# A hybrid decoder step on one core: the mixer's branches in another order, and its vector work in smaller steps

## Chip, core and metric

The kernel runs on one core of a Trainium2 chip. The metric is the device time of one execution in microseconds. Before the change three runs gave 2646.72, 2648.06 and 2648.72; the median is 2648.06.

## What is computed

One inference step of a two-layer trunk over 512 prompt tokens and 8 sequences of 8 sample tokens (576 columns), width 1024, in fp32. Each layer has a SwiGLU half step, a mixer and a second SwiGLU half step, each behind an RMS norm with scale and shift from a conditioning vector. The mixer, cut to what matters:

```python
xa, bg, cg, u, v, p, ga, gb, gc = split(h @ w_in)
y_a = (bg * conv3(concat(hist, cg * xa))) @ w_out_a              # conv branch
v   = layernorm(gelu(v)) * ln_g
y_b = (gelu(u) * (tril(w_s) @ v + b_s)) @ w_out_b                # gated MLP, chunks of 128
y_c = grouped(trailing_mean_w(p) - p) * pool_scale               # pool, w = 2, 4, 8, 16
out = (sigmoid(ga) * y_a + sigmoid(gb) * y_b + sigmoid(gc) * y_c) @ w_o
```

New conv, pool and v rows are outputs too.

## The kernel before

Activations lie with features on partitions and the 576 tokens as two halves of 288 columns (256 prompt, 32 sample). Every fp32 product is made of three fast ones: each operand is split into a rounded high part and the remainder, and `wlo*hi`, `whi*lo`, `whi*hi` are summed in a PSUM bank (lines 474 to 477). Five banks rotate first in, first out.

A **unit** (`units`, line 464) is one output tile of 128 x 288: its matmuls, then its evacuation, then `beat()`. A **group** (`Groups.group`, line 736) makes four output tiles by a scheme of seven products of 12 matmuls instead of eight; the bank of each product is copied or added by ScalarE (`pd`, `pe`, `pu`) and VectorE, and the seventh product, the tail, is issued within the next group or by `flush`. After each product `gone()` runs one `beat()`, one step of weight preparation (`W.go`) and a `tick`.

The order of the work is the order of the program: each engine takes its instructions in turn. Two lists delay work: `later(n, f)` runs `f` n beats on, and `after(n, f)` n ticks on (a product counts half a tick). So a step that waits for another engine holds back all that stands behind it on its own engine.

Weights come by DMA from the SP queue in pieces of up to 1 MB into two raw buffers, in the order of the list `raws` (lines 162 to 234), and are split ahead of use into six slots. A piece for a group needs two sums on GpSimd (L366, L362), two differences on VectorE (L362) and four splits (ScalarE L325, then VectorE L329). Other pieces are split by ScalarE and VectorE, every third by GpSimd (L323, L329), by a running count.

The mixer (`mixer`, line 995) does, per layer: v and u with layernorm (each 128-token block is transposed into a bank, normalised by VectorE with a power on GpSimd, and multiplied by `ln_g`); then the gated MLP: gate groups GB and, between them, outputs (`ypair`), whose evacuation starts the accumulator `acc`; then conv: groups XA, CG, BG, gate groups GA and outputs whose product is added to `acc` by GpSimd (L1163); then pool: groups PP, and gate groups GC0, GC2, GC4, GC6, between whose products the pool outputs `yc` (three matmuls each) are placed by `hook`. Each pool output is multiplied by its gate (L1440), added to `acc` (L1444) and split into `mgh` (ScalarE, L1446) and `mgl` (VectorE, L1447), which feed the product with `w_o` in `end_stage`. During a mixer the residual x lies in DRAM; its buffers hold split operands of the groups, and x is read back (L1480) at the mixer's end. While `pool_w` is in use its slot (`pw`) is not free.

Of the kernel before, what the change touches and what calls it, by code (L numbers as in the profile page):

```python
# [35 lines left out]
def kernel(  # L36
# [113 lines left out]
    colc = cp.tile([P, 88], F32, name="colc")  # L150
# [57 lines left out]
    for l in range(DEPTH):  # L208
        add_ffn(w1_gu[l], w1_dn[l], CHUNKS[l][0])
        wi = w_in[l]  # L210
        for c in (VV, VV + 256, UU, UU + 256):
            add_cols(wi, c, KT)
        for g, out in ((GB, w_out_b[l]), (GA, w_out_a[l])):
            if g == GA:
                for c in (XA, CG, XA + 256, CG + 256, BG, BG + 256):
# [9 lines left out]
        add_st(wi, PP)  # L225
        add_st(wi, PP + 256)
        add_st(wi, GC)
        add_pool(pool_w[l])
        add_st(wi, GC + 256)
        add_st(wi, GC + 512)  # L230
        add_st(wi, GC + 768)
# [232 lines left out]
    def units(specs, hooks={}, late=False, w=1):  # L464
# [23 lines left out]
        beat()  # L488
# [506 lines left out]
    def mixer(l, nxt):  # L995
# [36 lines left out]
        def layernorm(n):  # L1032
# [13 lines left out]
            rs = tmp("bnrs", 1, 2)  # L1046
            nc.vector.tensor_scalar_add(rs[:R], mv[:R, 1:2], EPS)
            nc.gpsimd.tensor_tensor(out=rs[:R], in0=rs[:R], in1=mhalf[:R, :1], op=ALU.pow)
            t = vn[n] = alloc(F32, "vn")
            nc.vector.tensor_scalar(t[:R, :512], bk[:R], mv[:R, 0:1], rs[:R], ALU.subtract, ALU.mult)  # L1050
            nc.vector.tensor_mul(t[:R, :512], t[:R, :512], lng[:R, :512])
            if n == 4:
                nc.sync.dma_start(o_nv[l].rearrange("b t c -> (b t) c"), t[:64, :512])
                release(vs, lng, *[v[m] for m in range(4)])
# [51 lines left out]
        def gating(hp):  # L1106
# [8 lines left out]
            for e in range(2):  # L1115
# [7 lines left out]
            nc.vector.tensor_add(  # L1123
                tg3[:, :, :PH].rearrange("p h (n t) -> p h n t", n=2),
                bk.rearrange("p (h n t) -> p h n t", h=2, n=2),
                bc.unsqueeze(1).unsqueeze(1).to_broadcast([P, 2, 2, P]))
# [30 lines left out]

        def evac_ya(m, h):
            def e(ps):
                t = sg.pop((m, h))  # L1160
                nc.vector.tensor_mul(t, ps[:, :HALF], t)
                a = acc[m][:, h * HALF:(h + 1) * HALF]
                nc.gpsimd.tensor_add(a, a, t)  # L1163
                qrelease(t)
            return e

        def ypair(rhs, evac, m):
            s = W.take()
            for h in (0, 1):
                for i in (0, 1):  # L1170
# [13 lines left out]
        hsc = alloc(F32, "hsc")  # L1184
        nc.sync.dma_start(hsc[:16, :512], state_conv[l].rearrange("b k c -> (b k) c"))
# [8 lines left out]


        xa, ext, cv = {}, {}, {}
        exs = alloc(F32, "exs")
        exs4 = exs[:, :320].rearrange("p (m s t) -> p m s t", m=4, s=8)
        def conv_hist():
            bk = tpbank()  # L1200
            for m in range(4):
                nc.tensor.transpose(bk[:, m * 16:(m + 1) * 16], hsc[:16, m * P:(m + 1) * P],
                                    ident[:16, :16])
            nc.vector.tensor_copy(
                exs4[:, :, :, 0:2], bk[:, :64].rearrange("p (m s t) -> p m s t", m=4, s=8))
            release(hsc)

        after(2, conv_hist)
        ncol = tmp("ncol", 4 * 18, 1)
        ncol3 = ncol.rearrange("p (m c) -> p m c", m=4)  # L1210

        def evac_xa(m, h):
            def e(ps, own=None):
                if own is None:
                    own = qalloc("xa")
                    nc.scalar.activation(own, ps[:, :HALF], AF.Copy)
                xa[m, h] = own
            return e

        def evac_cg(m, h):  # L1220
            def e(ps, own=None):
                first = m not in ext
                if first:
                    ext[m] = alloc(F32, "ext")
                    nc.gpsimd.memset(ext[m][:, 0:2], 0.0)
                a = xa.pop((m, h))
                nc.vector.tensor_mul(ext[m][:, 2 + h * PH:2 + (h + 1) * PH], ps[:, :PH], a[:, :PH])
                nc.vector.tensor_mul(exs4[:, m, 4 * h:4 * h + 4, 2:10],
                                     ps[:, PH:HALF].rearrange("p (s t) -> p s t", s=4),
                                     a[:, PH:HALF].rearrange("p (s t) -> p s t", s=4))  # L1230
                qrelease(a)
                if own is not None:
                    qrelease(own)
                if not first:
                    conv(m)
            return e

        def conv(m):

            cv[m] = alloc(F32, "cv")  # L1240
            w = [colc[:, 48 + (l * 3 + k) * 4 + m:48 + (l * 3 + k) * 4 + m + 1] for k in range(3)]
            o = cv[m].rearrange("p (h c) -> p h c", h=2)[:, :, 0:PH]
            os_ = cv[m].rearrange("p (h c) -> p h c", h=2)[:, :, PH:HALF].rearrange(
                "p h (s t) -> p h s t", s=4)
            e_ = lambda k: ext[m][:, k:k + 512].rearrange("p (h c) -> p h c", h=2)
            s_ = lambda k: exs4[:, m, :, k:k + 8].rearrange("p (h s) t -> p h s t", h=2)

            def tap0():
                nc.scalar.activation(o, e_(0), AF.Copy, scale=w[0])
                nc.vector.tensor_scalar_mul(os_, s_(0), w[0])  # L1250

            def tap(k):
                nc.vector.scalar_tensor_tensor(out=o, in0=e_(k), scalar=w[k], in1=o,
                                               op0=ALU.mult, op1=ALU.add)
                nc.vector.scalar_tensor_tensor(out=os_, in0=s_(k), scalar=w[k],
                                               in1=os_, op0=ALU.mult, op1=ALU.add)

            def last():
                nc.gpsimd.tensor_copy(ncol3[:, m, 0:2], ext[m][:, 512:514])
                nc.gpsimd.tensor_copy(ncol3[:, m, 2:18].rearrange("p (s t) -> p s t", s=8),  # L1260
                                      exs4[:, m, :, 8:10])
                release(ext[m])

            tap0()
            later(1, lambda: tap(1))
            later(2, lambda: (tap(2), last()))

        yah, yal, cvn = {}, {}, {}

        def evac_bg(m, h):  # L1270
            def e(ps, own=None):
                if m not in yah:
                    yah[m], yal[m] = alloc(F32R, "yah"), alloc(F32R, "yal")
                g = qalloc("g32") if own is None else own
                c = slice(h * HALF, (h + 1) * HALF)
                nc.vector.tensor_mul(g, ps[:, :HALF], cv[m][:, c])
                cvn[m] = cvn.get(m, 0) + 1
                if cvn[m] == 2:
                    release(cv[m])
                hi, lo = yah[m][:, c], yal[m][:, c]  # L1280

                def low():
                    nc.vector.tensor_sub(lo, g, hi.bitcast(F32))
                    qrelease(g)

                def high():
                    nc.scalar.activation(hi, g, AF.Copy)
                    later(1, low)
                later(1, high)
            return e  # L1290

        def out_conv():
            bk = tpbank()
            for m in range(4):
                nc.tensor.transpose(bk[:18, m * P:(m + 1) * P], ncol3[:, m, :], ident)
            t = alloc(F32, "ncv")
            nc.scalar.activation(t[:18, :512], bk[:18], AF.Copy)
            nc.sync.dma_start(o_ncp[l, 0], t[0:2, :512])
            nc.sync.dma_start(o_ncs[l].rearrange("b k c -> (b k) c"), t[2:18, :512])
            release(t)  # L1300

        for m in (0, 2):
            G.group(evac_xa, m)
            G.group(evac_cg, m)
        after(5.5, out_conv)
        G.group(evac_bg, 0)
# [542 lines left out]
```

## Time and profile before

| | us |
|---|---|
| median of three runs | 2648.06 |
| profiled execution | 2651.93 |
| its span | 2650.2 |
| TensorE busy | 2531.8 |
| VectorE busy | 1815.5 |
| ScalarE busy | 1125.9 |
| GpSimd busy | 867.5 |
| mean granted clock | 0.983 |

A share of the whole span is a mean over stages. The stages of the two mixers are read from windows: the first mixer's lie between 485 and 924 us, the second's between 1783 and 2225. The clock column there is the granted share of TensorE's full clock.

### The profile page before, as it was taken

What the parts mean: (1) busy time and instruction counts of PE and PEld (TensorE: products, weight loads), DVE (VectorE), ACT (ScalarE), POOL (GpSimd) and SP (SyncE); (2) the same over time, 40 slices, a digit from 0 to 9 for tenths busy, and PEclk for the clock granted to TensorE, in tenths of its full rate; (3) what the DMA queues carried; (4) which work ended last, traced back from release to release, by engine and by line L of the source; (5) the groups of instructions that cost most, each with busy time, mean ns of one, the idle gap of its engine ahead of it and who ended that gap; (6) DMA issues with size and microseconds to landing.
All of it is one profiled execution on the core that took longest, in us unless ns stands there. A gap on an engine that the chain in (4) does not pass through costs nothing. (4 is left out here: it accounts for less than half of the span.)

```text
span 2650.2 us, 46656 instructions
## 1 busy us (share of the span) xinstructions
PE 2531.8 (96%) x18604; PEld 2423.4 (91%) x18604; DVE 1815.5 (69%) x3167; ACT 1125.9 (42%) x2094; POOL 867.5 (33%) x942
## 2 busy tenths in 40 slices
PE   7999999999997999999999999999999879999998
PEld 5889999889997889999989999998999879999998
DVE  5766666766868586666776666767686765776675
ACT  4434334444444263334444344444444443453453
POOL 1223334312243323333443332452122514233241
PEclk8999999999999999999999999999999989999999
DMA  7554533312222424442324444241223231132222
GB/s 230 195 182 157 191 104 130 94 63 88 84 88 68 147 73 149 153 151 96 112 81 160 163 159 148 85 132 63 89 80 107 66 136 48 64 100 91 97 76 80
DMA packets 264761, 303.51 MB, mean 115 GB/s; under 512 B 10957, under 2 KB 224253, under 8 KB 264527
## 3 DMA queue, kind: packets, MB, share of 16 engines
q1 hardware_dynamic: 264542, 300.52, 34.2%
q8 instruction: 147, 2.41, 0.4%
q14 instruction: 72, 0.58, 0.1%
HBM read 292.74 MB, written 7.97 MB: 113 GB/s over the span
## 5 line engine op out<-in xcount | busy, mean ns | idle before, releaser
L329 DVE TENSOR_TENSOR wlo<-raw,whi 128x1024 fp32r<-128x1024 f32 (+2 forms) x548 | 631.8, 1161 | 231.0 <-ACT whi L325 222.4
L727 PE MATMUL mm<-hhi,wlo 128*128 128x288 f32 x1920 | 575.1, 300 | 35.0 <-ACT pe L765 34.2
L325 ACT ACTIVATE whi<-raw 128x1024 fp32r<-128x1024 f32 (+2 forms) x548 | 467.6, 861 | 318.4 <-PE mm L477 115.7
L728 PE MATMUL mm<-hlo,whi 128*128 128x288 f32 x1920 | 569.8, 297 | 0.0
L729 PE MATMUL mm<-hhi,whi 128*128 128x288 f32 x1920 | 569.7, 297 | 0.0
L727 PEld LDWEIGHTS mm<-hhi,wlo 128*128 128x128 f32 x1920 | 363.0, 189 | 61.4 <-ACT pe L765 39.3
L474 PE MATMUL mm<-ghi,wlo 128*128 128x288 f32 x1408 | 418.5, 297 | 0.0
L477 PE MATMUL mm<-ghi,whi 128*128 128x288 f32 x1408 | 415.1, 295 | 0.0
L476 PE MATMUL mm<-glo,whi 128*128 128x288 f32 x1408 | 414.8, 295 | 0.0
L729 PEld LDWEIGHTS mm<-hhi,whi 128*128 128x128 f32 x1920 | 363.1, 189 | 0.0
L728 PEld LDWEIGHTS mm<-hlo,whi 128*128 128x128 f32 x1920 | 363.1, 189 | 0.0
L727 PE MATMUL mm<-thi,wlo 128*128 128x288 f32 x1120 | 332.6, 297 | 1.6 <-ACT pd L754 1.6
L728 PE MATMUL mm<-tlo,whi 128*128 128x288 f32 x1120 | 330.3, 295 | 0.0
L729 PE MATMUL mm<-thi,whi 128*128 128x288 f32 x1120 | 329.5, 294 | 0.0
L366 POOL TENSOR_TENSOR whi<-raw 128x512 f32<-128x512 f32 x120 | 171.8, 1432 | 480.2 <-DMA raw<-in_w_in_dram 189.8
L802 DVE SCALAR_TENSOR_TENSOR x<-mm,mod,x 128x256 f32<-128x256 f32 x336 | 161.2, 480 | 222.4 <-PE mm L477 222.3
L474 PEld LDWEIGHTS mm<-ghi,wlo 128*128 128x128 f32 x1408 | 264.3, 188 | 17.8 <-issue 16.8
L476 PEld LDWEIGHTS mm<-glo,whi 128*128 128x128 f32 x1408 | 264.2, 188 | 0.2
L477 PEld LDWEIGHTS mm<-ghi,whi 128*128 128x128 f32 x1408 | 264.2, 188 | 0.0
L727 PEld LDWEIGHTS mm<-thi,wlo 128*128 128x128 f32 x1120 | 210.1, 188 | 14.1 <-issue 5.0
L729 PEld LDWEIGHTS mm<-thi,whi 128*128 128x128 f32 x1120 | 210.6, 188 | 0.0
L810 POOL TENSOR_TENSOR x<-x,t 128x32 f32<-128x32 f32 x240 | 112.2, 468 | 300.3 <-DVE t L805 297.8
(316 smaller groups left out, 4949.4 us busy)
## 6 DMA issues: line engine op xcount, KB each, us to landing
raw<-in_w_gu_dram SPq DMA_DIRECT2D x88, 1024.0 KB
ada<-in_w_ada_dram SPq DMA_DIRECT2D x256, 256.0 KB
raw<-in_w_in_dram SPq DMA_DIRECT2D x48, 1024.0 KB
raw<-in_w_dn_dram SPq DMA_DIRECT2D x52, 512.0 KB
raw<-in_w_dn_dram SPq DMA_DIRECT2D x24, 768.0 KB
adap<-in_w_ada_dram SPq DMA_DIRECT2D x32, 256.0 KB
raw<-in_w_o_dram SPq DMA_DIRECT2D x8, 1024.0 KB
xd<-x SPq DMA_DIRECT2D x16, 288.0 KB
```

The lines of the kernel that those rows point to most:

```text
L325: nc.scalar.activation(hi, src, AF.Copy)
L329: eng.tensor_sub(lo, src, hi.bitcast(F32))
L366: nc.gpsimd.tensor_add(v4(self.sums[r][0])[:, 0], a21, a22)
L474: nc.tensor.matmul(o, wlo, rhi, start=(k == 0), stop=False)
L476: nc.tensor.matmul(o, whi, rlo, start=False, stop=False)
L477: nc.tensor.matmul(o, whi, rhi, start=False, stop=(k == K - 1 and not late))
L727: nc.tensor.matmul(o, wlo, rhi, start=(start and k == 0), stop=False, skip_group_check=True)
L728: nc.tensor.matmul(o, whi, rlo, start=False, stop=False, skip_group_check=True)
L729: nc.tensor.matmul(o, whi, rhi, start=False, stop=(k == 3), skip_group_check=True)
L802: nc.vector.scalar_tensor_tensor(out=xc, in0=ps[:, :PH], scalar=mod[:, gidx + m, 0:1], in1=xc, op0=ALU.mult, op1=ALU.add)
L810: (nc.gpsimd if late else nc.vector).tensor_add(xs, xs, t)
```

## The change

The order of the branches becomes gated MLP, pool, conv; the weight list follows. Layernorm's scaling is done by ScalarE one beat after the statistics, and `ln_g` is multiplied in at the gating, as a column, for the prompt blocks. The split of the gated result is made in two later beats. Pool outputs no longer count as beats (`still`) and are added to `acc` by GpSimd; the last four are placed in the first conv group. The conv outputs add `acc` on GpSimd and make `mgh` and `mgl` in three beats. x is read back before the last eight conv outputs. The four outputs of a `ypair` come tile by tile instead of half by half.

```diff
-            nc.vector.tensor_scalar(t[:R, :512], bk[:R], mv[:R, 0:1], rs[:R], ALU.subtract, ALU.mult)
-            nc.vector.tensor_mul(t[:R, :512], t[:R, :512], lng[:R, :512])
...
+            def scale():
+                nc.vector.scalar_tensor_tensor(out=rs[:R, 1:2], in0=mv[:R, 0:1], scalar=-1.0,
+                                               in1=rs[:R, 0:1], op0=ALU.mult, op1=ALU.mult)
+                t = vn[n] = alloc(F32, "vn")
+                nc.scalar.activation(t[:R, :512], bk[:R], AF.Identity, scale=rs[:R, 0:1],
+                                     bias=rs[:R, 1:2])
...
+            later(1, scale)
```

Gating:

```diff
-            nc.vector.tensor_add(
-                tg3[:, :, :PH].rearrange("p h (n t) -> p h n t", n=2),
...
+            for h in range(2):
+                nc.vector.scalar_tensor_tensor(
+                    out=tg3[:, h, :PH].rearrange("p (n t) -> p n t", n=2),
+                    in0=bk[:, h * PH:(h + 1) * PH].rearrange("p (n t) -> p n t", n=2),
+                    scalar=colc[:, 88 + l * 4 + hp:88 + l * 4 + hp + 1],
+                    in1=bc.unsqueeze(1).to_broadcast([P, 2, P]), op0=ALU.mult, op1=ALU.add)
...
-            nc.scalar.activation(ybh[hp], tg, AF.Copy)
-            nc.vector.tensor_sub(ybl[hp], tg, ybh[hp].bitcast(F32))
-            release(tg)
+            def low():
+                nc.vector.tensor_sub(ybl[hp], tg, ybh[hp].bitcast(F32))
+                release(tg)
+            def high():
+                nc.scalar.activation(ybh[hp], tg, AF.Copy)
+                later(1, low)
+            later(1, high)
```

Conv outputs and pool outputs:

```diff
         def evac_ya(m, h):
...
-                a = acc[m][:, h * HALF:(h + 1) * HALF]
-                nc.gpsimd.tensor_add(a, a, t)
-                qrelease(t)
+                def add():
+                    nc.gpsimd.tensor_add(t, t, acc[m][:, c])
...
+                def high():
...
+                    nc.scalar.activation(mgh[m][:, c], t, AF.Copy)
+                def low():
+                    nc.vector.tensor_sub(mgl[m][:, c], t, mgh[m][:, c].bitcast(F32))
+                    qrelease(t)
+                for n, f in enumerate((add, high, low)):
+                    later(n + 1, f)
...
         def evac_yc(m, h):
...
-                nc.vector.tensor_add(t, t, a)
-                hi = mgh[m][:, h * HALF:(h + 1) * HALF]
-                nc.scalar.activation(hi, t, AF.Copy)
-                nc.vector.tensor_sub(mgl[m][:, h * HALF:(h + 1) * HALF], t, hi.bitcast(F32))
-                qrelease(t)
+                def add():
+                    a = acc[m][:, h * HALF:(h + 1) * HALF]
+                    nc.gpsimd.tensor_add(a, a, t)
+                    qrelease(t)
+                later(1, add)
```

Order, with the conv part moved behind the pool part:

```diff
+        def last_yc(n):
+            hook(6)(n)
+            if n == 6:
+                W.done(pw)
         for m in (0, 2):
-            G.group(evac_xa, m)
+            G.group(evac_xa, m, last_yc if m == 0 else lambda n: None)
             G.group(evac_cg, m)
...
         G.group(evac_g, 6)
-        ypair(ra, evac_ya, 4)
-        G.flush()
-        ypair(ra, evac_ya, 6)
+        G.flush()
+        t_free()
+        in_x[0] = False
         for q in range(4):
             xq[q] = x_room(q)
         for m in range(KT):
             nc.sync.dma_start(xv(m, slice(0, NTOK)), xd[l][:, m, :])
-        yc(6, 0)
-        yc(6, 1)
-        G.flush()
-        yc(7, 0)
-        yc(7, 1)
-        W.done(pw)
-        drain()
-        t_free()
-        in_x[0] = False
+        ypair(ra, evac_ya, 4)
+        ypair(ra, evac_ya, 6)
...
+        drain()
```

The columns of `ln_g` are loaded at the start with the other small columns by one DMA more.

## Rows read from the trace of the kernel before

**Rows 1.** The page: busy time, share and instructions of each engine.
```profile
PE 2531.8 (96%) x18604; PEld 2423.4 (91%) x18604; DVE 1815.5 (69%) x3167; ACT 1125.9 (42%) x2094; POOL 867.5 (33%) x942
```

**Rows 2.** Waits of TensorE, whole run: us in total, times, longest us.
```profile
PE mm L727 <- ACT pe L765: 34.2, 18, 5.5
PE mm L727 <- DVE pd L1440: 17.4, 6, 4.0
...
PE tpb L1063 <- DVE vn L1050: 4.4, 3, 1.9
...
PE tpb L1038 <- DVE vn L1050: 2.2, 3, 1.2
...
PE tpb L1041 <- DVE vn L1050: 1.6, 2, 0.8
```

**Rows 3.** Windows: length, busy of PE, PEld, DVE, ACT, POOL, clock, DMA share, GB/s.
```profile
629.89:703.10 73.21, 69.83 (x504) 69.17 (x503) 64.62 (x102) 34.68 (x55) 18.71 (x22) 0.95 0.27 88
703.10:776.49 73.39, 72.01 (x541) 71.63 (x540) 44.96 (x62) 29.95 (x51) 26.75 (x23) 1.00 0.29 90
776.49:813.09 36.60, 32.99 (x246) 32.51 (x245) 32.43 (x48) 18.87 (x40) 22.20 (x29) 1.00 0.31 101
813.09:923.51 110.42, 93.53 (x634) 91.29 (x633) 70.50 (x127) 38.97 (x72) 28.50 (x28) 0.91 0.33 110
2069.56:2109.91 40.35, 34.85 (x246) 34.42 (x245) 34.70 (x48) 18.14 (x40) 27.11 (x32) 0.92 0.29 92
2109.91:2224.61 114.70, 95.75 (x635) 92.94 (x633) 69.75 (x126) 38.73 (x72) 26.69 (x27) 0.90 0.29 97
```

**Rows 4.** Timeline of TensorE: start, us, engine, line, operation, tiles, shape.
```profile
2069.56 0.29 PE L727 MATMUL mm<-hhi,wlo 128*128 128x288 f32 x1
...
2072.76 0.57 PE L1339 MATMUL tpb<-ident,hsp 120*128 120x120 f32 x4
```

**Rows 5.** Window of a half-clock piece, columns as in rows 3.
```profile
694.29:701.11 6.82, 5.69 (x24) 5.69 (x25) 5.91 (x10) 3.51 (x7) 0.00 (x0) 0.50 0.49 159
```

**Rows 6.** Timeline of VectorE, last row TensorE, pool outputs; in brackets idle before.
```profile
832.93 1.22 DVE L329 TENSOR_TENSOR wlo<-whi,whi 128x1024 fp32r<-128x1024 f32 x1
834.07 0.51 DVE L1440 SCALAR_TENSOR_TENSOR sg<-mm,colc,sg 128x288 f32<-128x288 f32 x1
...
835.58 0.46 DVE L1447 TENSOR_TENSOR mgl<-sg,mgh 128x288 fp32r<-128x288 f32 x1 [0.51 <-ACT mgh L1446]
...
841.26 0.61 PE L727 MATMUL mm<-x,wlo 128*128 128x288 f32 x1 [3.95 <-DVE pd L1440]
```

**Rows 7.** Timeline of GpSimd in the second mixer's pool start.
```profile
2097.32 2.65 POOL L329 TENSOR_TENSOR wlo<-raw,whi 128x1024 fp32r<-128x1024 f32 x1
```

**Rows 8.** Timeline of the SP queue at the start.
```profile
3.01 0.34 SPq L1584 DMA_DIRECT2D small<-in_pool_scale_dram  x1
```

**Rows 9.** Timeline of TensorE in conv.
```profile
695.42 0.61 PE L727 MATMUL mm<-hhi,wlo 128*128 128x288 f32 x1 [3.38 <-ACT pe L765]
```

**Rows 10.** Timeline of VectorE, last row ScalarE, in layernorm.
```profile
523.73 0.81 DVE L1050 TENSOR_SCALAR vn<-tpb,bnmv,bnrs 128x512 f32<-128x512 f32 x1 [5.77 <-POOL bnrs L1048]
...
532.91 0.81 DVE L1050 TENSOR_SCALAR vn<-tpb,bnmv,bnrs 128x512 f32<-128x512 f32 x1 [0.73 <-POOL bnrs L1048]
533.75 0.69 DVE L1051 TENSOR_TENSOR vn<-vn,lng 128x512 f32<-128x512 f32 x1
...
540.27 0.60 ACT L1065 ACTIVATE ws<-tpb 128x512 f32<-128x512 f32 x1 [1.07 <-PE tpb L1063]
```

**Rows 11.** Timeline of TensorE in the gating stage.
```profile
571.43 0.40 PE L727 MATMUL mm<-hhi,wlo 128*128 128x288 f32 x1 [1.56 <-ACT pe L765]
```

**Rows 12.** Groups by shape: busy us, mean ns of one, idle before.
```profile
L1253 DVE SCALAR_TENSOR_TENSOR cv<-ext,colc,cv 128x512 f32<-128x512 f32 x16 | 16.8, 1047 | 4.2 <-ACT cv L1249 4.2
...
L1163 POOL TENSOR_TENSOR acc<-acc,pe 128x288 f32<-128x288 f32 x8 | 13.7, 1716 | 5.2 <-DVE pe L1161 5.2
...
L1163 POOL TENSOR_TENSOR acc<-acc,pu 128x288 f32<-128x288 f32 x8 | 6.5, 807 | 2.2 <-DVE pu L1161 2.2
```

More of the change, by code (lines that the diff above doesn't have):

```diff
@@ L214 @@
             if g == GA:
-                for c in (XA, CG, XA + 256, CG + 256, BG, BG + 256):
+                for c in (PP, PP + 256, GC):
+                    add_st(wi, c)
+                add_pool(pool_w[l])
+                for c in (GC + 256, GC + 512, GC + 768,
+                          XA, CG, XA + 256, CG + 256, BG, BG + 256):
                     add_st(wi, c)
@@ L224 @@
             add_out(out, 768)
[L225 to L231, printed above, removed]
         for m in range(0, 8, 2):
@@ L462, in flush, with units @@
             pend.pop(0)[1]()
-    def units(specs, hooks={}, late=False, w=1):
+    def units(specs, hooks={}, late=False, w=1, still=False):
         bk = [balloc() for _ in specs]
@@ L487, in units @@
             brelease(b)
-        beat()
+        if not still:
+            beat()
         tick(len(specs) * w)
@@ L1045, in layernorm @@
             nc.vector.bn_aggr(out=mv[:R], in_=st[:R])
[L1046 to L1049, printed above, removed]
-            nc.vector.tensor_scalar(t[:R, :512], bk[:R], mv[:R, 0:1], rs[:R], ALU.subtract, ALU.mult)
-            nc.vector.tensor_mul(t[:R, :512], t[:R, :512], lng[:R, :512])
-            if n == 4:
-                nc.sync.dma_start(o_nv[l].rearrange("b t c -> (b t) c"), t[:64, :512])
-                release(vs, lng, *[v[m] for m in range(4)])
+            rs = tmp("bnrs", 2, 2)
+            nc.vector.tensor_scalar_add(rs[:R, 0:1], mv[:R, 1:2], EPS)
+            nc.gpsimd.tensor_tensor(out=rs[:R, 0:1], in0=rs[:R, 0:1], in1=mhalf[:R, :1], op=ALU.pow)
+            def scale():
[4 more added lines that the diff above has]
+                                     bias=rs[:R, 1:2])
+                if n == 4:
+                    nc.vector.tensor_mul(t[:R, :512], t[:R, :512], lng[:R, :512])
+                    nc.sync.dma_start(o_nv[l].rearrange("b t c -> (b t) c"), t[:64, :512])
+                    release(vs, lng, *[v[m] for m in range(4)])
+            later(1, scale)
         ws = {}
@@ L1156, in evac_yb @@
             return e
+        mgh, mgl, macc = {}, {}, {}
         def evac_ya(m, h):
@@ L1168, in ypair @@
             s = W.take()
-            for h in (0, 1):
-                for i in (0, 1):
+            for i in (0, 1):
+                for h in (0, 1):
                     units([(s, 4 * i, 4, rhs(h), evac(m + i, h))])
@@ L1193, in mixer @@
             release(ybh[k], ybl[k])
[L1196 to L1302, printed above, removed]
-            G.group(evac_xa, m)
-            G.group(evac_cg, m)
@@ L1320, in mixer @@
-        G.group(evac_g, 6)
-        ypair(ra, evac_ya, 4)
-        G.flush()
-        ypair(ra, evac_ya, 6)
-        for k in range(4):
-            release(yah[k], yal[k])
         xp = {}
@@ L1431, in out_pool @@
             qrelease(ptail, pcol, *xps)
-        mgh, mgl = {}, {}
         def evac_yc(m, h):
             def e(ps):
-                if h == 0:
-                    mgh[m], mgl[m] = alloc(F32R, "mgh"), alloc(F32R, "mgl")
                 t = sg.pop((m, h))
@@ L1476, in mixer, with conv_hist @@
         G.group(evac_g, 6, hook(4))
+        hsc = alloc(F32, "hsc")
+        nc.sync.dma_start(hsc[:16, :512], state_conv[l].rearrange("b k c -> (b k) c"))
+        xa, ext, cv = {}, {}, {}
+        exs = alloc(F32, "exs")
+        exs4 = exs[:, :320].rearrange("p (m s t) -> p m s t", m=4, s=8)
+        def conv_hist():
+            bk = tpbank()
+            for m in range(4):
+                nc.tensor.transpose(bk[:, m * 16:(m + 1) * 16], hsc[:16, m * P:(m + 1) * P],
+                                    ident[:16, :16])
+            nc.vector.tensor_copy(
+                exs4[:, :, :, 0:2], bk[:, :64].rearrange("p (m s t) -> p m s t", m=4, s=8))
+            release(hsc)
@@ new lines, in mixer, with evac_xa, e, evac_cg @@
+        after(1, conv_hist)
+        ncol = tmp("ncol", 4 * 18, 1)
+        ncol3 = ncol.rearrange("p (m c) -> p m c", m=4)
+        def evac_xa(m, h):
+            def e(ps, own=None):
+                if own is None:
+                    own = qalloc("xa")
+                    nc.scalar.activation(own, ps[:, :HALF], AF.Copy)
+                xa[m, h] = own
+            return e
+        def evac_cg(m, h):
+            def e(ps, own=None):
+                first = m not in ext
+                if first:
+                    ext[m] = alloc(F32, "ext")
+                    nc.gpsimd.memset(ext[m][:, 0:2], 0.0)
+                a = xa.pop((m, h))
+                nc.vector.tensor_mul(ext[m][:, 2 + h * PH:2 + (h + 1) * PH], ps[:, :PH], a[:, :PH])
+                nc.vector.tensor_mul(exs4[:, m, 4 * h:4 * h + 4, 2:10],
+                                     ps[:, PH:HALF].rearrange("p (s t) -> p s t", s=4),
+                                     a[:, PH:HALF].rearrange("p (s t) -> p s t", s=4))
+                qrelease(a)
+                if own is not None:
+                    qrelease(own)
+                if not first:
+                    conv(m)
+            return e
@@ new lines, in conv, with tap0, tap, last @@
+        def conv(m):
+            cv[m] = alloc(F32, "cv")
+            w = [colc[:, 48 + (l * 3 + k) * 4 + m:48 + (l * 3 + k) * 4 + m + 1] for k in range(3)]
+            o = cv[m].rearrange("p (h c) -> p h c", h=2)[:, :, 0:PH]
+            os_ = cv[m].rearrange("p (h c) -> p h c", h=2)[:, :, PH:HALF].rearrange(
+                "p h (s t) -> p h s t", s=4)
+            e_ = lambda k: ext[m][:, k:k + 512].rearrange("p (h c) -> p h c", h=2)
+            s_ = lambda k: exs4[:, m, :, k:k + 8].rearrange("p (h s) t -> p h s t", h=2)
+            def tap0():
+                nc.scalar.activation(o, e_(0), AF.Copy, scale=w[0])
+                nc.vector.tensor_scalar_mul(os_, s_(0), w[0])
+            def tap(k):
+                nc.vector.scalar_tensor_tensor(out=o, in0=e_(k), scalar=w[k], in1=o,
+                                               op0=ALU.mult, op1=ALU.add)
+                nc.vector.scalar_tensor_tensor(out=os_, in0=s_(k), scalar=w[k],
+                                               in1=os_, op0=ALU.mult, op1=ALU.add)
+            def last():
+                nc.gpsimd.tensor_copy(ncol3[:, m, 0:2], ext[m][:, 512:514])
+                nc.gpsimd.tensor_copy(ncol3[:, m, 2:18].rearrange("p (s t) -> p s t", s=8),
+                                      exs4[:, m, :, 8:10])
+                release(ext[m])
+            tap0()
+            later(1, lambda: tap(1))
+            later(2, lambda: (tap(2), last()))
@@ new lines, in mixer, with evac_bg, e, low @@
+        yah, yal, cvn = {}, {}, {}
+        def evac_bg(m, h):
+            def e(ps, own=None):
+                if m not in yah:
+                    yah[m], yal[m] = alloc(F32R, "yah"), alloc(F32R, "yal")
+                g = qalloc("g32") if own is None else own
+                c = slice(h * HALF, (h + 1) * HALF)
+                nc.vector.tensor_mul(g, ps[:, :HALF], cv[m][:, c])
+                cvn[m] = cvn.get(m, 0) + 1
+                if cvn[m] == 2:
+                    release(cv[m])
+                hi, lo = yah[m][:, c], yal[m][:, c]
+                def low():
+                    nc.vector.tensor_sub(lo, g, hi.bitcast(F32))
+                    qrelease(g)
+                def high():
+                    nc.scalar.activation(hi, g, AF.Copy)
+                    later(1, low)
+                later(1, high)
+            return e
@@ new lines, in out_conv @@
+        def out_conv():
+            bk = tpbank()
+            for m in range(4):
+                nc.tensor.transpose(bk[:18, m * P:(m + 1) * P], ncol3[:, m, :], ident)
+            t = alloc(F32, "ncv")
+            nc.scalar.activation(t[:18, :512], bk[:18], AF.Copy)
+            nc.sync.dma_start(o_ncp[l, 0], t[0:2, :512])
+            nc.sync.dma_start(o_ncs[l].rearrange("b k c -> (b k) c"), t[2:18, :512])
+            release(t)
+        def last_yc(n):
+            hook(6)(n)
+            if n == 6:
+                W.done(pw)
@@ new lines, in mixer, with ra @@
+        for m in (0, 2):
+            G.group(evac_xa, m, last_yc if m == 0 else lambda n: None)
+            G.group(evac_cg, m)
+        after(5.5, out_conv)
+        G.group(evac_bg, 0)
+        G.group(evac_bg, 2)
+        release(exs)
+        def ra(h):
+            return lambda k: (yah[k][:, h * HALF:(h + 1) * HALF], yal[k][:, h * HALF:(h + 1) * HALF])
+        G.group(evac_g, 0)
+        G.group(evac_g, 2)
+        ypair(ra, evac_ya, 0)
+        G.group(evac_g, 4)
+        ypair(ra, evac_ya, 2)
@@ L1477, in mixer @@
+        G.group(evac_g, 6)
+        G.flush()
+        t_free()
+        in_x[0] = False
         for q in range(4):
@@ L1480, in mixer @@
             nc.sync.dma_start(xv(m, slice(0, NTOK)), xd[l][:, m, :])
-        yc(6, 0)
-        yc(6, 1)
-        G.flush()
-        yc(7, 0)
-        yc(7, 1)
-        W.done(pw)
+        ypair(ra, evac_ya, 4)
+        ypair(ra, evac_ya, 6)
+        for k in range(4):
+            release(yah[k], yal[k])
         drain()
-        t_free()
-        in_x[0] = False
         def rm(h):
```

41 lines of the change are left out of this document (15 added, 26 removed).

## Prediction

> **What bounds the kernel now.** I read the page first: TensorE (PE) is busy 96% of the span [rows 1], so speed elsewhere is worth only what PE waits for it. Next the waits of PE over the whole run [rows 2]: products wait for ScalarE's bank copy `pe` (34.2 us) and for VectorE's evacuation of the pool outputs, L1440 (17.4 us), and layernorm's transposes for `vn` (4.4 + 2.2 + 1.6 = 8.2 us). Then the windows of the mixers by stage [rows 3]. At full clock a 288-column matmul starts every 0.133 us: 24 of them lie between 2069.56 and 2072.76 [rows 4]. That gives each stage its time without waits. From the first product of gate group GC2 to the next norm (813.09 to 923.51, and 2109.91 to 2224.61) there are by the code 22 products of 12 matmuls, 16 pool outputs of 3 and 13 units of 24: 624 x 0.133 = 83.2 us, and 0.9 us of transposes: 84.1. It took 110.4 and 114.7, so 26.3 + 30.6 = 56.9 us are lost there, partly waiting and partly at the low clock that follows a wait: granted 0.91 and 0.90 in the mean; a half-clock piece has 24 matmuls in 5.69 us, 0.237 each [rows 5], so a usual fall of 3.4 us costs 3.4 x 0.44 = 1.5. The 20 products before it need 32.3 us and took 36.6 and 40.35: 12.3 us lost. Conv has one wait of 3.4 us per mixer. The stage from 703 to 776, gates and conv outputs, loses next to nothing; VectorE (DVE) is busy 45 of 73 us there, but 64.6 of 73.2 in conv.
>
> **Why the pool outputs stall** [rows 6]. Each one costs DVE the product L1440 (0.51), an add (0.46, as the remainder), a wait for ScalarE's `mgh` (0.51) and the remainder L1447 (0.46): 1.94 us, four per group, 7.8 us. A group's weight splits take three pieces of 1.22 and three of half the size (0.69, as L1051 takes for 512 columns, with its row at layernorm), 5.7 us of DVE, and its three bank adds 1.4. That is 14.9 us of DVE against 7 x 1.6 + 4 x 0.4 = 12.8 us of PE: DVE falls behind, banks come back late, and PE stands (3.95 us at 841.26).
>
> **The change, part by part.** Durations are those of the profiled execution (2651.93 us, span 2650.2); the gain is taken from the median, 2648.06, which lies 3.9 us lower.
>
> *Order and merged split.* PE's work is the same, only moved. A pool output keeps L1440 alone on DVE; its add goes to GpSimd (POOL), and `mgh`, `mgl` move to the conv outputs, where DVE gets 16 x 0.46 = 7.4 us and ScalarE about as much more in a stage with 28 us of DVE idle. A gate group then asks DVE for 5.7 + 1.4 + 2.0 = 9.1 us in 12.8 of PE. What is left of the 56.9 us: the first pool output (a wait near 3 us in one mixer, near 2 in the other) sits behind the same pool steps and splits as before, so it stays, with one clock fall: 6.5. `still` takes the extra beats away, the pool means come a beat later, and the transposes of the pool tails wait some 0.6 us each: 1.2. At 841 the queue ahead of L1440 loses 2 x 1.43 us, so about 1 of 3.95 stays, in both mixers: 2. The mixer now ends on conv outputs: product 0.46, POOL add 0.8 (row in rival A), ScalarE and DVE 0.46 each, spread over the outputs that follow; the half that the next product's first unit reads last is due some 0.3 us late: 1 for both. POOL and DVE colliding: 2. Sum 13, so this part gives **44** (between 25 and 57).
> The weight queue: the count that sends every third split to POOL reaches `pool_w` four splits earlier. Counted through the code it was 60th in the first mixer (on DVE) and 173rd in the second (on POOL [rows 7], where the longest `pe` wait of all, 5.5 us, follows); now 56th and 169th, so POOL cuts it in the first mixer and DVE in the second. The loss changes places: 0. The refetch of x goes out some 13 us ahead of its first use but behind two weight loads: 0, at most 5 per mixer if these hold it back. The conv state is fetched one group before its transposes instead of far ahead: 0, at most 3 per mixer. The tail product that now precedes the last four outputs needs a split that was done ten us earlier in this place: 0.
>
> *Conv after pool.* Its first group now carries four pool outputs (2.0 us of DVE) and weight splits that lag by some three steps (`pw` holds a slot), where DVE had about 4 us of idle to lose. The wait at 695 [rows 9] stays, and I add 2 us a mixer: **-4** (0 to -12).
>
> *Layernorm* [rows 10]. DVE no longer waits in line for POOL's root (0.73 each) and loses 0.81 + 0.69 per block; ScalarE scales from the bank a unit later (nearest row: its 128x512 bank copy, 0.60). The first root still comes late from POOL (DVE waited 5.77 for it), so about 1.2 of the 8.2 us stays, and one clock fall of 1.5 after the last wait goes: 8.5, I take **8** (3 to 10).
>
> *Gating.* Two half-width operations replace one over 512 columns: some +0.2 on DVE each, hidden by PE. ScalarE no longer stands before DVE's product with `pe` behind it, so the 1.56 us wait at 571.43 [rows 11] goes in both mixers; but the next split waits for its weights and the last gating still ends as the first output starts, so I take half: **1.6** (-1 to 3).
>
> *Small ones.* One more DMA issue ahead of the input's (0.34 for its neighbour [rows 8]): -0.4. Conv outputs with more work on three engines: -1 (0 to -4).
>
> Sum: 44 + 8 + 1.6 - 4 - 0.4 - 1 = 48, and 2648 - 48 = **2600 us**.
>
> **Rivals.**
> *A. GpSimd's adds give the gain back.* Of the four adds of a group of conv outputs three take 0.81 us and the one that meets DVE's split 1.72 [rows 12]. From GC2 through the first conv group PE needs 51.2 us and DVE 4 x 7.1 + 16 x 0.51 + 3 of pool steps = 39.5, so 11.7 are spare. If each of 16 adds holds DVE for its 0.8 us, 12.9 go: nothing is spare, conv starts with a backlog that it can't work off, and each of four groups has a wait of about 2 us with a clock fall, 14 a mixer, and 2 more in conv: 32 of the 48 are lost, 2632. Against it: L1440 reads a bank and stays at 0.51, and the add and the remainder that go had both inputs in SBUF as well. The Trainium skill ("SBUF — State Buffer", Who interferes with whom) says that a VectorE instruction with two SBUF inputs and a GpSimd instruction that reads SBUF exclude each other for the whole instruction. By that rule 0.8 us would be the price of every add that meets a split, and this rival would stand; the rows agree for one add in four.
> *B. Slower: DVE becomes the bound of one long stretch.* Pool, gates and conv now follow each other without the conv outputs between, in which DVE catches up. From the first pool group to the last conv group PE has 12 x 11.2 + 6.4 + 0.8 = 141.6 us, DVE by unstretched rows 12 x 7.1 + 14 (pool) + 8 (outputs) + 14 (conv) + 7 (products with B) + 2 = 130. PE waits from a stretch of 1.09 on. At 1.4, near what the conv taps show (1.05 us in the mean [rows 12], against 0.69 for the other 512-column product of rows 10), DVE takes 182: 40 us lost a mixer and some 9 at low clock, 98 in all against 79 lost there now (56.9 + 12.3 + 10 in conv), so 19 slower, less the 9.6 of layernorm and gating: 2657. Against it: over the conv stage DVE was busy 64.6 us for about 60 of unstretched rows, a stretch of 1.08.
> *C. No change:* the `pe` waits (34.2 us) take up whatever the outputs leave, since ScalarE stands behind the same DVE. For it: they are the largest row. Against it: they come where DVE is late, and DVE is relieved.
>
> **How the numbers follow.** Forecast (gain 36 to 62: 2586 to 2612) 0.67; A (gain 10 to 36) 0.22; B 0.05; C 0.03; a gain above 62 0.03. The 80% range runs from 2586 to A's 2632. A measurement of this kernel tells 0.2% (5 us) from no change: faster 0.91, same 0.03, slower 0.06.
>
> **What would show it.** Right: no wait on L1440 after the first pool output of each mixer; a granted clock of 0.97 or more from GC4 to the norm; no wait for `mgh`; waits for `vn` near 1 us in all; the 5.5 us wait in the first mixer's pool start. A: splits over 1.5 us beside POOL's adds in the gate groups. B: waits for ScalarE's `pe` in every conv group. Wrong: over 2 us at the transposes of the pool tails or of the conv state, or the next product's first unit waiting for `mgl`.

## Result and profile after

The changed kernel takes **2603.32 us** (median of four, 2601.91 to 2607.70) against 2648.39 for the kernel before beside it: ratio 0.9829, 95% interval 0.981 to 0.9848. Run a second time in another set it took 2609.93 against 2651.55: 0.9845 (0.9831 to 0.986). So the gain is 42 to 45 us where 48 were forecast. The kernel before lay between 2648.2 and 2651.6 from set to set; kernels are therefore compared by their ratio to it in the same set, or by stretches of their profiled executions.

The page of the changed kernel, its first line (it answers to [rows 1]):

```profile
PE 2511.0 (96%) x18604; PEld 2405.1 (92%) x18604; DVE 1796.3 (69%) x3135; ACT 1134.4 (44%) x2104; POOL 901.7 (35%) x974
```

TensorE has the same 18604 matmuls; what became shorter is the time around them and the part at the low clock. VectorE has 32 instructions less and GpSimd 32 more, as many as there are additions of pool outputs.

Waits of TensorE over the whole run (answers to [rows 2]; L763 was L765, L1335 was L1440, L1052 was L1050):

```profile
PE mm L725 <- ACT pe L763: 28.6, 13, 5.6
PE mm L725 <- DVE pe L776: 8.9, 3, 6.9
...
PE mm L725 <- DVE pd L1335: 3.6, 3, 1.8
...
PE tpb L1036 <- ACT vn L1052: 2.8, 2, 2.6
...
PE mm L473 <- DVE mgl L1191: 1.7, 1, 1.7
PE tpb L1317 <- POOL ptail L1298: 1.5, 1, 1.5
```

Waits for the pool outputs' product fell from 17.4 us on the largest row alone to 3.6, those for `vn` from 8.2 to 2.8. A row rose: `pe` L776, VectorE's addition behind a group's sixth product, 0.8 us before, is now 8.9, nearly all of it in one wait of 6.9.

Windows by stage (answers to [rows 3], same columns), for each mixer: pool start; gate groups with pool outputs; conv with the last four pool outputs; gates with conv outputs; the first 13 units of the merge up to the norm.

```profile
620.66:660.92 40.26, 34.70 (x246) 34.17 (x245) 34.08 (x48) 18.56 (x40) 20.57 (x29) 0.92 0.29 92
660.92:704.13 43.21, 39.94 (x299) 39.05 (x298) 33.38 (x48) 21.69 (x38) 22.40 (x23) 1.00 0.26 81
704.13:780.72 76.59, 72.31 (x526) 70.85 (x525) 68.52 (x107) 35.32 (x56) 27.97 (x30) 0.98 0.26 84
780.72:858.45 77.73, 72.48 (x542) 71.77 (x541) 52.58 (x73) 35.42 (x66) 29.97 (x24) 1.00 0.41 138
858.45:901.71 43.26, 41.55 (x315) 41.32 (x313) 18.81 (x46) 10.73 (x20) 13.28 (x14) 1.00 0.30 101
1896.30:1934.37 38.07, 34.42 (x247) 33.88 (x246) 31.94 (x49) 19.14 (x41) 17.81 (x26) 0.96 0.30 97
1934.37:1977.85 43.48, 41.48 (x298) 40.55 (x297) 33.64 (x48) 21.80 (x38) 22.61 (x24) 0.96 0.26 81
1977.85:2053.73 75.88, 71.82 (x526) 70.79 (x525) 67.83 (x107) 35.43 (x57) 28.19 (x30) 0.98 0.26 85
2053.73:2138.23 84.50, 74.23 (x542) 73.52 (x541) 54.20 (x75) 37.17 (x68) 27.18 (x23) 0.96 0.38 128
2138.23:2179.51 41.28, 41.28 (x315) 41.28 (x313) 19.31 (x44) 9.07 (x17) 15.43 (x15) 1.00 0.24 79
```

The same windows of the kernel before for conv and for gates with conv outputs, in both mixers:

```profile
629.89:702.85 72.96, 69.58 (x503) 68.92 (x502) 64.37 (x102) 34.43 (x55) 18.71 (x22) 0.95 0.27 88
702.85:776.49 73.64, 72.26 (x543) 71.88 (x542) 45.21 (x62) 30.20 (x51) 26.75 (x23) 1.00 0.29 90
1924.18:1994.60 70.42, 67.05 (x503) 66.39 (x502) 62.74 (x100) 32.53 (x51) 18.69 (x22) 1.00 0.28 91
1994.60:2069.56 74.96, 72.34 (x543) 71.87 (x541) 45.55 (x64) 31.86 (x54) 27.63 (x23) 1.00 0.28 88
```

The 110.4 and 114.7 us at clock 0.91 and 0.90 from the second gate group to the norm have become 43.21 + 43.26 and 43.48 + 41.28 at 0.96 to 1.00. The gates with conv outputs went the other way: 73.64 to 77.73 and 74.96 to 84.50. Where this 84.50 comes from, in the timeline of the second mixer's last gate group (TensorE's row last; in brackets the idle time before):

```profile
2114.02 1.06 ACT L322 ACTIVATE whi<-raw 128x1024 fp32r<-128x1024 f32 x1 [3.65 <-DMA raw<-in_w_o_dram]
...
2118.21 2.34 POOL L326 TENSOR_TENSOR wlo<-raw,whi 128x1024 fp32r<-128x1024 f32 x1
...
2118.46 3.17 DVE L326 TENSOR_TENSOR wlo<-raw,whi 128x1024 fp32r<-128x1024 f32 x1 [1.75 <-ACT whi L322]
2121.56 0.45 DVE L776 TENSOR_TENSOR pe<-mm,pe 128x288 f32<-128x288 f32 x1
...
2122.06 0.61 PE L725 MATMUL mm<-hhi,wlo 128*128 128x288 f32 x1 [6.87 <-DVE pe L776]
```

The matmul at 2122.06 is the last group's tail product. It adds into the bank in which the sixth product has just ended; VectorE must read that result first (L776), and stands in a weight split that takes 3.17 us beside GpSimd's of 2.34. The split is not the whole of the 6.87 us: VectorE had stood 1.75 us for its high part, which ScalarE made late, having itself stood 3.65 us for the weights of w_o (first row). In the first mixer the reading addition (843.53 us) came ahead of the next split (845.69 us), and the wait was 1.40.

### The profile page after: what moved, and what is told of

Its sections match the earlier page's. It is cut to its first block, busy times and chain, and to the rows that moved or that the text cites. A ratio compares the mean times of both kernels' runs of the same rounds, so it can differ in the third digit from the quotient of the medians.

```text
span 2606.0 us, 46663 instructions
## 1 busy us (share of the span) xinstructions
PE 2511.0 (96%) x18604; PEld 2405.1 (92%) x18604; DVE 1796.3 (69%) x3135; ACT 1134.4 (44%) x2104; POOL 901.7 (35%) x974
## 5 line engine op out<-in xcount | busy, mean ns | idle before, releaser
L326 DVE TENSOR_TENSOR wlo<-raw,whi 128x1024 fp32r<-128x1024 f32 (+2 forms) x548 | 639.2, 1174 | 238.4 <-ACT whi L322 230.5
L363 POOL TENSOR_TENSOR whi<-raw 128x512 f32<-128x512 f32 x120 | 177.6, 1480 | 418.8 <-DMA raw<-in_w_in_dram 166.6
```

What stands on the lines that cost most here:

```text
L326: eng.tensor_sub(lo, src, hi.bitcast(F32))
L363: nc.gpsimd.tensor_add(v4(self.sums[r][0])[:, 0], a21, a22)
```

## Experiments

Mixer lengths below run from the norm's wait for `accsq` at the mixer's start to the one after its merge (in the changed kernel 481.08 to 917.25 and 1760.02 to 2195.07), in the profiled execution.

| kernel | median us | ratio to before in its set (95%) | mixer 1 | mixer 2 |
|---|---|---|---|---|
| before | 2648.4 to 2651.6 | 1 | 454.14 | 457.59 |
| changed | 2603.32 | 0.9829 (0.981-0.9848) | 436.17 | 435.05 |
| changed again | 2609.93 | 0.9845 (0.9831-0.986) | 437.55 | 434.79 |
| tail later | 2601.84 | 0.982 (0.9806-0.9833) | 436.39 | 429.70 |
| refetch later | 2606.42 | 0.9837 (0.9823-0.985) | 436.17 | 437.21 |
| pool_w on ScalarE | 2605.13 | 0.9836 (0.9822-0.9849) | 434.45 | 433.46 |
| adds on VectorE | 2609.05 | 0.9851 (0.9838-0.9865) | 436.54 | 433.94 |
| order only | 2617.94 | 0.9878 (0.9864-0.9892) | 440.89 | 439.78 |
| gating at once | 2611.92 | 0.9855 (0.9841-0.9868) | 438.95 | 436.51 |
| four edits | 2593.05 | 0.9785 (0.9771-0.9799) | 428.52 | 424.88 |
| copies later | 2592.71 | 0.979 (0.9773-0.9808) | 432.96 | 423.96 |
| adds twice | 2620.15 | 0.9899 (0.9882-0.9917) | 441.87 | 440.37 |

"Tail later", "refetch later", "pool_w on ScalarE" and "adds on VectorE" are one set; "changed again", "order only", "gating at once" and "four edits" another; "copies later" and "adds twice" a third.

**Changed again.** 

> The changed kernel itself, unaltered, beside the others: 2603 us. Its spread over five runs says how far medians of five can be told apart; by the four runs so far (2601.9 to 2607.7) about 2 us.


It took 6.6 us more than in its first set, 3.2 of them shared by the kernel before; the mixers agree within 1.4 us. Differences of medians below some 4 us between sets say nothing here.

**Tail later.**
```diff
         G.group(evac_g, 6)
-        G.flush()
         t_free()
...
         ypair(ra, evac_ya, 4)
+        G.flush()
         ypair(ra, evac_ya, 6)
```


> The last group's tail product goes back behind the first four of the last eight conv outputs. Theory 'tail': that product adds into the bank which VectorE's addition of `pe` must have read first, and stands directly behind the product whose result that is; VectorE is held by a weight split, so TensorE stood 1.40 us in the first mixer and 6.87 us in the second, the latter followed by a piece at half clock. With 4 products of 12 matmuls (4 x 1.6 = 6.4 us) between the two, both waits go, and the clock fall with them: 8 to 11 us faster than the changed kernel, 2594 us. Rival 'transfer': VectorE is late because the weights of w_o land late, and it is as late for the conv outputs' evacuation; the wait only moves to a conv output or to the tail in its new place: a gain of 0 to 3 us, 2601 us or more, with a wait over 4 us left within 10 us of the old one.


Both waits are gone; of the second mixer's gates and conv outputs, 2050 to 2140 us, one row of waits is left in this kernel:

```profile
PE mm L725 <- ACT pe L763: 2.8, 1, 2.8
```

No wait took their place in the second mixer, which became 5.4 us shorter. The first mixer became no shorter, though its 1.40 us went: the merge's wait for `mgl` rose from 1.71 to 2.18, and this time a low clock followed it. The clock is the number behind the busy times; in the changed kernel both windows stand at 1.00:

```profile
860.00:865.00 5.00, 3.29 (x25) 1.00 0.17 46
865.00:870.00 5.00, 5.00 (x40) 1.00 0.49 167
```

With the tail later they do not:

```profile
860.00:865.00 5.00, 2.83 (x16) 0.85 0.38 119
865.00:870.00 5.00, 5.00 (x33) 0.81 0.27 94
```

The mechanism is shown. Late weights alone do not make the wait: in this run too ScalarE stood 2.95 us for those of w_o (at 2115.63 us). The 8 to 11 us expected were too much, the traces give 5, and the time alone doesn't tell it from zero.

**Refetch later.**
```diff
-        for q in range(4):
-            xq[q] = x_room(q)
-        for m in range(KT):
-            nc.sync.dma_start(xv(m, slice(0, NTOK)), xd[l][:, m, :])
         ypair(ra, evac_ya, 4)
+        for q in range(4):
+            xq[q] = x_room(q)
+        for m in range(KT):
+            nc.sync.dma_start(xv(m, slice(0, NTOK)), xd[l][:, m, :])
         ypair(ra, evac_ya, 6)
```


> The refetch of x is issued after the first four of the last eight conv outputs and not ahead of them; the tail product stays where the change put it. Theory 'tail': the order of the transfers is not what decides, the wait of 6.87 us in the second mixer stays above 4 us: within 3 us of the changed kernel, 2603 us. Rival 'transfer': the refetch's eight transfers delay the weights of w_o, for which ScalarE and then VectorE wait; without them ahead the second mixer's wait falls under 2 us and the 2.6 to 2.9 us waits for ScalarE's `pe` shrink: 6 to 9 us faster, 2596 us. Against both: x itself may come late for the first products after the norm's start, up to 5 us slower.


The wait stays, at 6.1 us, so the order of these transfers is not its cause. The changed kernel's trace says so by itself: there too the refetch is issued only at 2128.44 us, behind the loads of w_o and after the wait has ended at 2122.06. So this run could not move the wait, and is no test of what else delays these weights. Waits of the second mixer, 2050 to 2140 us, in this run:

```profile
PE mm L725 <- DVE pe L776: 6.1, 1, 6.1
PE mm L725 <- ACT pe L763: 3.8, 2, 2.7
```

**pool_w on ScalarE.**
```diff
-        add_raw(dma, [(lambda t: t[:, :1024], lambda s: s, None)])
+        add_raw(dma, [(lambda t: t[:, :1024], lambda s: s, "AD")])
```


> pool_w is split by ScalarE and VectorE in both mixers; all other splits stay where they were counted. Theory 'who splits pool_w': the wait of 5.57 us at the start of the first mixer's gates comes from GpSimd's split of that tensor, since the second mixer, where VectorE splits it, waits 2.72 us there: 3 us less and a clock fall shortened, 3 to 5 us faster than the changed kernel, 2599 us. Rival: VectorE is late there from the pool steps whoever splits it, and the wait stays at 4 us or more: within 1.5 us.


Waits in the first mixer, 640 to 662 us, in the changed kernel:

```profile
PE mm L725 <- ACT pe L763: 5.6, 1, 5.6
```

And in this one:

```profile
PE mm L725 <- ACT pe L763: 2.8, 1, 2.8
PE mm L725 <- ACT pd L752: 0.9, 1, 0.9
```

The long wait follows GpSimd's split, as the theory said. It is worth 1.7 to 3.1 us of the first mixer; the time doesn't resolve it.

**Adds on VectorE, adds twice.**
```diff
-                    nc.gpsimd.tensor_add(a, a, t)
+                    nc.vector.tensor_add(a, a, t)
```


> The additions of the pool outputs, 16 per mixer, run on VectorE and not on GpSimd, in the same place of the order. By the forecast's count VectorE is asked for 9.1 + 4 x 0.46 = 10.9 us in a group of 12.8 us of TensorE, still not the bound, but the first conv group gets no slack back: 0 to 8 us slower than the changed kernel, 2606 us. By the rival of the forecast (each GpSimd addition holds VectorE for its own 0.8 us) the additions cost VectorE 0.46 and not 0.8 once they are its own: 2 to 6 us faster, 2599 us.


```diff
                     nc.gpsimd.tensor_add(a, a, t)
+                    nc.gpsimd.tensor_add(t, t, a)
```


> The changed kernel with a second GpSimd addition of two SBUF halves behind each of the 16 pool-output additions of a mixer (its result is not used). By the forecast's rival A each addition that meets VectorE's splits holds it for its own 0.8 us: 16 x 0.8 = 13 us more of VectorE's time per mixer where it has 12 to spare, 10 to 25 us slower, 2620 us or more, with splits over 1.5 us in the gate groups. By the forecast itself (collisions 2 us in all) doubling them costs 0 to 4 us: 2607 us.


With the additions on VectorE the mixers are as long as with GpSimd's, within 1 us; by the time it is 0.1 to 0.2% slower, which the intervals don't tell from nothing. Doubling GpSimd's costs 10 to 11 us in the mixers (441.87 + 440.37 against 871.22 and 872.34), 14 by the ratios of 0.9899 and 0.9845: more than the forecast's view allowed and within the rival's 10 to 25. Windows of the gate groups with pool outputs and of conv, in the changed kernel's second run:

```profile
663.36:706.60 43.24, 40.11 (x300) 39.21 (x299) 33.41 (x48) 21.71 (x38) 22.41 (x23) 1.00 0.26 81
706.60:783.20 76.60, 72.35 (x527) 70.97 (x527) 68.67 (x108) 35.75 (x58) 27.88 (x30) 0.98 0.26 84
```

And with the additions doubled:

```profile
661.20:708.00 46.80, 41.63 (x307) 40.28 (x306) 37.05 (x47) 21.48 (x37) 32.63 (x33) 1.00 0.24 75
708.00:787.00 79.00, 72.23 (x516) 69.65 (x515) 71.89 (x109) 35.22 (x57) 35.10 (x36) 0.98 0.25 81
```

VectorE has the same work and is busy 3.6 and 3.2 us longer in them: 16 more GpSimd additions put 6.9 us on VectorE, 0.43 each, as much as an addition of its own (0.46). This 0.43 is a mean over all sixteen, not the price of one meeting. The Trainium skill ("SBUF — State Buffer", Who interferes with whom) lets a VectorE instruction with two SBUF inputs and a GpSimd instruction that reads SBUF exclude each other for the whole instruction. Taken pair by pair the changed kernel's trace agrees, and the one that starts second pays:

```profile
680.10 0.81 POOL L1341 TENSOR_TENSOR acc<-acc,sg 128x288 f32<-128x288 f32 x1 [7.28 <-DVE sg L1335]
680.36 1.63 DVE L326 TENSOR_TENSOR wlo<-raw,whi 128x1024 fp32r<-128x1024 f32 x1
680.86 1.78 POOL L1341 TENSOR_TENSOR acc<-acc,pe 128x288 f32<-128x288 f32 x1
```

The split met 0.55 us of the first addition and took 0.41 more than its usual 1.22. The second addition met 1.13 us of the split and took 0.97 more than 0.81. In these pairs VectorE pays only where GpSimd started first.

**Order only.**
```diff
...
-                nc.scalar.activation(t[:R, :512], bk[:R], AF.Identity, scale=rs[:R, 0:1],
-                                     bias=rs[:R, 1:2])
...
-            later(1, scale)
...
+            nc.vector.tensor_scalar(t[:R, :512], bk[:R], mv[:R, 0:1], rs[:R], ALU.subtract, ALU.mult)
+            nc.vector.tensor_mul(t[:R, :512], t[:R, :512], lng[:R, :512])
...
-            later(1, high)
+            nc.scalar.activation(ybh[hp], tg, AF.Copy)
+            nc.vector.tensor_sub(ybl[hp], tg, ybh[hp].bitcast(F32))
...
```


> The changed kernel with layernorm and gating as they were before: order of the branches, merged split and pool steps alone. In the traces of before and after the stretch from the mixer's first norm to the first output of the MLP branch shrank from 94.86 to 89.61 us and from 91.52 to 86.04 us, 10.7 us in both mixers. If the parts add up, this kernel takes 10.7 us more than the changed one, 2614 us, 34 less than before, and the `vn` waits of before return. Rival: what layernorm gives is taken back downstream (splits then late, a clock fall elsewhere): 4 us or less more than the changed one, 2607 us. By the forecast's own terms (8 + 1.6) it would be 2613 us.


It costs 8.0 us in the same set (2617.94 against 2609.93), and the `vn` waits of before are back (480 to 600 us):

```profile
PE tpb L1061 <- DVE vn L1048: 2.5, 2, 2.0
PE tpb L1036 <- DVE vn L1048: 2.0, 2, 1.3
```

So the kernel without the layernorm and gating parts is 33.6 us faster than before, and these parts give 8.0 on top of it. What they give without the rest of the change was not tried, so that the parts add up is not shown.

**Gating at once.**
```diff
...
-            later(1, high)
+            nc.scalar.activation(ybh[hp], tg, AF.Copy)
+            nc.vector.tensor_sub(ybl[hp], tg, ybh[hp].bitcast(F32))
+            release(tg)
```


> The changed kernel, but gating issues ScalarE's `ybh` and VectorE's `ybl` directly behind its product again and not a product apart each. Theory: ScalarE then waits for VectorE's gating product with `pe` queued behind it, and the wait of before at the gates (1.56 us in each mixer, before a group's matmuls, ended by `pe`) returns, while the wait of 1.23 us at the first output for `ybh` shrinks by a third to a half: 1 to 3 us slower, 2605 us. Rival: the split across products delays `ybh` of the last gating by as much as it saves: within 1 us or faster.


The wait for `pe` at the gates returns, from 555 to 600 us the only one:

```profile
PE mm L725 <- ACT pe L763: 2.0, 1, 2.0
```

In exchange the waits at the first output (1.23 + 0.40) are gone. The mixers are 1.4 and 1.7 us longer than in the changed kernel's run of this set, and the time 2.0, which its intervals don't tell from nothing.

**Four edits.** The tail later, pool_w on ScalarE, and:
```diff
-        after(2, out_pool)
+        after(2.5, out_pool)
...
                     units([(s, 4 * i, 4, rhs(h), evac(m + i, h))])
+            last()
             W.done()
...
```
(`last` is `drain` for the last pair of conv outputs and does nothing for the others.)


> The changed kernel with four edits: the tail product behind the first four of the last eight conv outputs, pool_w split by ScalarE and VectorE, the transposes of the pool tails one product later, and the last merged remainders issued ahead of the next weight split. If the waits are independent they add up: 5 us (tail, as the trace of its run shows within the mixers) + 3 (pool_w) + 3 (two waits of 1.5 us for `ptail`) + 2 (waits of 1.7 us for `mgl`, shortened by the split's 1.2) = 13 us faster than the changed kernel, 2590 us. Rival: waits behind the same late VectorE and weight transfers take each other's place, and the clock falls come at another wait: 3 to 6 us, 2598 us.


16.9 us faster than the changed kernel in the same set, with no overlap of the runs (2590.97 to 2595.29 against 2605.88 to 2611.56): 58.5 faster than before. That is more than the sum of 13 and far above the rival's 3 to 6. The waits for the tail, `ptail` and `mgl` are gone or under 0.8 us.

**Copies later.** On top of the four edits:
```diff
-            for n, f in enumerate([double] * (i + 1) + [mean, high, low]):
+            for n, f in enumerate([double] * (i + 1) + [mean, lambda: None, high, low]):
...
-                later(1, high)
+                later(2, high)
```
(the second edit is in the conv gates)


> The kernel with the four edits, and ScalarE's copies `plh` (pool means) and `yah` (conv gates) issued one product later than there, since in the traces ScalarE stood before them (6.1 us for GpSimd's `pl`, 4.0 us for VectorE's `pe`) with the bank copy `pe` queued behind. Theory: the two waits of TensorE that end with that `pe` (2.7 us at the start of the gates, 3.37 us in conv, in both mixers) fall under 1 us each, 8 to 10 us with what the clock gives back, less 1 to 2 us because the first pool output comes later: 2585 us. Rival: VectorE is more than a product behind there, so ScalarE's `pe` is not what ends last; the next bank or the first pool output waits instead: within 3 us of the four edits, 2592 us.


No gain: the first mixer became 4.4 us longer, the second 0.9 shorter. Waits of the first mixer, 640 to 790 us, with the four edits:

```profile
PE mm L725 <- ACT pe L763: 7.1, 3, 3.4
PE mm L725 <- DVE pd L1336: 3.1, 1, 3.1
PE mm L725 <- ACT pd L752: 1.3, 2, 0.9
```

And with the copies later:

```profile
PE mm L725 <- ACT pe L763: 6.3, 3, 3.0
PE mm L725 <- DVE pd L1336: 2.6, 1, 2.6
PE mm L725 <- ACT pd L752: 2.2, 2, 1.2
```

What `pe` gives (0.8) the next bank copy `pd` takes (0.9), so shifting ScalarE's queue frees nothing. This is what the rival forecast; its reason, that VectorE is more than a product behind there, fits the rows and was not tried by itself.

## Why the prediction held, and where it failed

Gains in the profiled executions, both mixers together, stretch by stretch:

- *First norm to the first MLP output*: 94.86 + 91.52 to 89.61 + 86.04, **10.7** against 8 + 1.6. With both parts undone 8.0 us of time are lost, so the terms had the right size. The first root still comes late, but costs 2.58 us in the first mixer and 0.2 in the second, instead of 1.2 altogether.
- *Pool start*: 36.60 + 40.35 [rows 3] to 40.26 + 38.07, **-1.4** against 0. The split of pool_w changed places as counted: the 5.57 us wait now stands in the first mixer.
- *Pool outputs and merge up to the norm*: 225.12 to 171.23. One product (1.6 us) and four outputs (1.6) per mixer moved into conv; without these 6.4 the gain is **47.5**, against 44. No pool output but the first waits (one more for 0.16 us), none for `mgh`; the transposes of the pool tails wait 1.5 us in the first mixer, not 0.6. The first product with `w_o` waits 1.71 us for `mgl` in the first mixer and not in the second; the prediction had put 1 for both into its 44, and named such a wait as a sign of being wrong.
- *Conv*: 72.96 + 70.42 to 76.59 + 75.88, less the 6.4 moved in: **-2.7** against -4. The wait of 3.4 stays.
- *Gates and conv outputs*: 73.64 + 74.96 to 77.73 + 84.50, **-13.6** against -1. This is the failed step: "The tail product that now precedes the last four outputs needs a split that was done ten us earlier in this place: 0." The split was there. What the product also needs is its bank, which VectorE has to read after the product directly ahead; the prediction asked for the operand and not for the accumulator. Waits of 1.40 and 6.87, some 2.0 lost at the low clock behind the second, and 2.6 more at the transfers of w_out_a (2.90 + 2.58 against 1.38 + 1.54) make 12.9. Why these transfers land later was not tried. The 2.0 is an estimate from this window, whose first 1.06 us still belong to the wait:

```profile
2121.00:2130.00 9.00, 7.94 (x46) 0.72 0.43 145
```

The sum is 40.5 of the 48.6 us forecast inside the mixers: the gates lost 12.6 more than their term, the other stages gave 4.5 more than theirs. A further 3.8 of the 44.2 us between the two profiled executions lie ahead of the first mixer, where nothing changed but one transfer: it starts at 481.08 us here (480.25 to 483.25 in the other runs) and at 484.92 before. No term of the prediction explains these 3.8; that they brought the total nearer to 48 is luck.

Rival A was half right: GpSimd's additions are not free, its sign (splits over 1.5 us) shows at 680.36 us, a further addition costs VectorE 0.43 us in the mean, what it would have paid itself, and moving them there bought nothing. But 0.8 us for each addition that meets a split was too much: where the split has started first, GpSimd pays. It did not take the gain back because without the remainders and the wait for `mgh` VectorE has slack in the gate groups (33.4 us busy of 43.2); that these two carry the gain is read from the windows and was not tried by itself. B and C did not occur.

## To carry to other kernels

When a product is moved, list everything that it waits for: its operands, and the readers of the bank into which it accumulates; a product that adds into a bank that was just evacuated halfway needs other work between. Of a change in several parts ask which carries the gain: here the engine that does the additions gave nothing, and the stage that VectorE was short in gave nearly all. Look which engine is late before shifting the queue of one that waits for it: here such a shift only renamed the wait.

## What the runs showed unexpectedly

- Of each four GpSimd additions of one shape, one takes more than twice as long, in the changed kernel as in the one before ([rows 12]). It is the one into `pe`'s half, as at 680.86 us above, where it starts while VectorE's split runs:

```profile
L1341 POOL TENSOR_TENSOR acc<-acc,pe 128x288 f32<-128x288 f32 x8 | 14.3, 1787 | 0.0
...
L1341 POOL TENSOR_TENSOR acc<-acc,sg 128x288 f32<-128x288 f32 x8 | 6.5, 811 | 49.3 <-DVE sg L1335 49.3
```

- VectorE's split took 3.17 us beside GpSimd's split of 2.34 that had started 0.25 us earlier, against 1.23 without it: 1.94 us more, of the 2.09 that GpSimd's still had to run. With the tail later VectorE started 0.23 us ahead, and it was GpSimd's that took longer:

```profile
2120.07 1.22 DVE L326 TENSOR_TENSOR wlo<-raw,whi 128x1024 fp32r<-128x1024 f32 x1 [1.75 <-ACT whi L322]
2120.30 3.26 POOL L326 TENSOR_TENSOR wlo<-raw,whi 128x1024 fp32r<-128x1024 f32 x1
```

- A wait's price depends on whether the clock falls behind it: 1.71 us at `mgl` was followed by a granted clock of 1.00, 2.18 us at the same place by 0.85 and 0.81, which took back what a wait ahead of it had given.
